# A hybrid decoder block on one core: conv gates multiplied at the convolution's results, the last mixing group in another order

## The chip, the cores and the metric

One Trainium2 chip, one core of it. The metric is the device time of one execution in microseconds (us); the time of a kernel is the median of several executions. The engines are named as in the profile: PE does the matrix products (PEld is its weight load), DVE and ACT work on tiles elementwise, POOL issues most of the kernel's own stores and reloads to and from DRAM, SP issues the loads of weights.

## What is computed

The reference is one layer over 512 tokens and a width of 2048, in float32:

```python
h = rmsnorm(x, g_mix)
cb, cc, cv, q, k, v, f_logit, gate_c, gate_a = split(h @ w_in)
conv_branch = (cb * causal_dwconv(cc * cv, conv_w)) @ w_conv_out
attn_branch = forgetting_attention(q, k, v, log_sigmoid(f_logit + b_f)) @ w_attn_out
merged = sigmoid(gate_c + b_c) * conv_branch + sigmoid(gate_a + b_a) * attn_branch
x = x + merged @ w_mix_out
h = rmsnorm(x, g_mlp)
x = x + square(relu(h @ w_ff1)) @ w_ff2
out = rmsnorm(x, g_final)
```

## The kernel before

**Products.** Every large operand is split into a rounded part and a remainder (`split`, L102: ACT writes the rounded part `th`, L103; DVE subtracts it to give `tl`, L104), and PE multiplies three of the four pairs. Most matrix products are done as seven half-size products in place of eight. A `Group` (L178) is one such product of a 512-column stretch of weights: `load` has SP fetch a quarter of the weights into one of four tiles `x0` to `x3`; `run` splits it into a `th` and a `tl` buffer (two of each, so one product ahead) and issues the matmuls, then calls what the dictionary `after` has for that product's name; `snap` is an ACT copy out of a PSUM bank and `plus` a DVE sum with one; `put(i, j, v)` takes a finished quarter (i: half of the tokens, j: half of the columns). `head` (L234) does the products A11 and A12 and puts quarter (0, 0); `tail2` (L291) does S1, S3, S2, S4 and A22 and puts (1, 1), (0, 1) and (1, 0). The weights' differences that S1 to A22 need are DVE subtractions (`sub`, L107).

**Stages around the change**, in the order of time. The gates are computed and stored to `g_d` (L757 to L777). Then come four column stretches c = 0 to 3 of the two branches. `conv_out(c)` (L871) is one `Group` with the convolution's result; before, its `put` (L873) stores each quarter to `held_d` in DRAM through POOL. `attn_out(c)` (L908) is a plain product in two chunks of 48 matmuls of 512 columns; its `cons_at` (L910) loads the attention gate `gt`, multiplies the PSUM result by it and adds that onto `merged[c]`. `bring(c)` (L891) makes the tile `merged[c]` (c below 3: the one tile `x1`), reloads the quarters from `held_d`, loads the conv gates `hg` into tiles of the ring "o" (five buffers, shared with `snap`'s copies and `gt`), and multiplies (`onto`, L882, with the DVE lines L885 and L889). `all_of(c)` (L925) makes the seven operands `M` of the mixing product from `merged[c]` (`quads`, L838), and then brings c + 1. The order is conv 0, attention 0 (with bring 0), conv 1, attention 1, conv 2, conv 3, attention 2, attention 3.

**Mixing** (L1061 to L1082) is four groups g = 0 to 3 with `M` as the token side. `Mix.put` (L984) adds x, takes squares, stores x1, and appends a `turn` (L996) to `waiting`: four PE transposes into a PSUM bank and ACT copies into `F`. `turn_waiting` (L1047) runs after certain products. In the last group the results also start the operands of the MLP: `begin_part(n, k)` (L961) reloads the first six eighths of an operand into tile `t<k>`, which is free once PE has done the products that read what lies there, `split_part` splits it, and `supply` adds a missing eighth.

**MLP, first half**: five groups begin with heads done early, and their five `tail2` come later (L1171 to L1192). The result's squares and sums are made by `sums(j)` in `put_u` (L1110): four ACT operations, five DVE operations and two POOL stores, with one buffer `r` and one `rh`, so each `sums` waits for the store of the one before. `sums(0)` is appended to `later`, and the next `tail2` runs what is in `later` (L309).

Each engine runs its instructions in the order of one list. A scheduler makes that list from the program, and the trace shows it departing from the written order (reloads and splits stand ahead of their place); an instruction that waits holds up all behind it on its engine.

Of the kernel before, what the change touches and what calls it, by code (L numbers as in the profile page):

```python
# [8 lines left out]
F32 = mybir.dt.float32  # L9
# [6 lines left out]
P = 128  # L16
# [29 lines left out]
def tile_hybrid_block(ctx: ExitStack, tc, x, g_mix, w_in, b_f, b_gate, conv_w, w_conv_out,  # L46
# [23 lines left out]
    def otile(shape, name, dt=F32):  # L70
        return main.tile(shape, dt, tag="o", name=name, bufs=5)
# [106 lines left out]
    class Group:  # L178

        def __init__(self, view, c1, c2, w, ST, mm, banks, put, scale=1.0, extra={}, after={}):
            self.extra, self.after = extra, after
            self.view, self.cs, self.w, self.ST, self.mm, self.banks = view, (c1, c2), w, ST, mm, banks
            self.put, self.scale, self.at = put, scale, {}
            self.nq = view.shape[0] // (2 * P)
# [11 lines left out]
            return [bank(i, which) for i in self.banks["abcd".index(which)]]  # L198

        def run(self, ps, n, src, first):  # L200
            hi, lo = parts([P, self.nq, self.w], SHIFT if self.w == HS else 0)
            split(src, hi, lo)
            if n in self.extra:
                self.mm(ps, self.ST(n), hi, lo, first, self.extra[n])
            else:
                self.mm(ps, self.ST(n), hi, lo, first)
            self.after.get(n, lambda: None)()
# [83 lines left out]
        def tail2(self):  # L291

            X = self.quarters((0, 1), (0, 0), (1, 1), (1, 0))
            a = self.a
            sub(X[0, 0], X[0, 1], X[0, 0])
            c = self.acc("c")
            self.run(c, "S1", X[0, 0], True)
            sub(X[0, 1], X[1, 1], X[0, 1])
            d = self.acc("d")
            self.run(d, "S3", X[0, 1], True)  # L300
            sub(X[0, 1], X[1, 1], X[0, 0])
            self.done(0, 0)
            d1 = self.snap(d, self.scale)
            self.plus(d1, c, self.scale)
            self.run(a, "S2", X[0, 1], False)
            sub(X[1, 0], X[1, 0], X[0, 1])
            self.done(0, 1)
            s2 = self.snap(a)
            while later:  # L309
                later.pop(0)()  # L310
            self.plus(d1, a, self.scale)
            self.put(1, 1, d1)
            self.run(c, "S4", X[1, 1], False)
            self.done(1, 1)
            s4 = self.snap(c, self.scale)
            self.plus(s4, a, self.scale)
            self.put(0, 1, s4)
            self.run(d, "A22", X[1, 0], False)
            self.done(1, 0)
            self.plus(s2, d)  # L320
            self.put(1, 0, s2)


    def eights(t, w=S):

# [544 lines left out]

    def conv_out(c, banks):  # L871

        def put(i, j, v):  # L873
            ts = slice(i * HS, (i + 1) * HS)
            nc.gpsimd.dma_start(out=held_d[c, 2 * j:2 * j + 2, :, ts].rearrange("k p s -> p k s"), in_=v)

        whole(Columns(w_conv_out, c * S, c * S + HS, HS, YS.get, mm_cols, tuple((b,) for b in banks), put,
                      extra={"A11": "first", "S3": "first"}))
# [3 lines left out]
    def onto(c, j, g, op):  # L882
# [3 lines left out]
        else:  # L886
            for h in range(2):
                o = merged[c][h][:, j % 2, j // 2, :]
                nc.vector.tensor_tensor(out=o, in0=o, in1=g[:, h * HS:(h + 1) * HS], op=op)  # L889

    def bring(c):  # L891

        if c < 3:
            t = main.tile([P, 2, 2, 2, HS], F32, tag="x1", name="merged")
            merged[c] = t[:, 0], t[:, 1]
            whole_of[c] = t
        else:
            merged[c] = [pm.tile([P, 2, 2, HS], F32, tag=f"f{i}", name="merged") for i in range(2)]
        for h in range(2):
            for par in range(2):  # L900
                nc.gpsimd.dma_start(out=merged[c][h][:, par], in_=held_d[c, par::2, :, h * HS:(h + 1) * HS].rearrange(
                    "j p s -> p j s"))
        for j in range(4):
            hg = otile([P, S], "hg")
            nc.gpsimd.dma_start(out=hg, in_=g_d[0, 4 * c + j])
            onto(c, j, hg, ALU.mult)

    def attn_out(c, banks, last=False, **how):  # L908

# [21 lines left out]
    M.place(4, [(n, 0) for n in ("A11", "A12", "S1", "S3")])  # L931
    M.place(6, [("S2", 0), ("S4", 0), ("A22", 0), ("A22", 1)])
    conv_out(0, lower)
    attn_out(0, upper, between={0: lambda: bring(0)})
    conv_out(1, lower)
    attn_out(1, upper, between={0: lambda: all_of(0)})
    conv_out(2, lower)
# [32 lines left out]
    class Mix:  # L970
# [25 lines left out]
        def turn(self, i, j, v):  # L996
            g = self.g
            k = 4 * g + 2 * j
            pt = bank(5 + (2 * i + j) % 3, "ptr").rearrange("p (two s) -> p two s", two=2)
            for par in range(2):  # L1000
                for t in range(2):
                    nc.tensor.transpose(pt[:, par, t * P:(t + 1) * P], v[:, t, par * P:(par + 1) * P], ident)
            gs = [gmlpT[:, k + par:k + par + 1] for par in range(2)]
            if self.last and i == 0:
                for par, n in enumerate(("A11", "A12")):
                    if n not in Q2:
                        self.missing.append((n, par, j))
                        continue
                    hi, lo = (Q2[n][:, e, 2 * g + j, :] for e in range(2))
                    nc.scalar.activation(out=hi, in_=pt[:, par, :], func=AF.Copy, scale=gs[par])  # L1010
                    nc.vector.scalar_tensor_tensor(out=lo, in0=pt[:, par, :], scalar=gs[par], in1=hi.bitcast(F32),  # L1011
                                                   op0=ALU.mult, op1=ALU.subtract)
            for par in range(2):
                nc.scalar.activation(out=self.F[i][:, par, j, :], in_=pt[:, par, :], func=AF.Copy, scale=gs[par])
            if (i, j) == (0, 1) and not self.last:
                for par, n in enumerate(("A11", "A12")):
                    self.out(n, self.F[0][:, par])
# [43 lines left out]
    for g in range(4):  # L1061
        mix = Mix(g)
        after = Steps()
        if g == 0:
            for n, n2 in zip(("A12", "S1", "S3", "S2", "S4"), ("S1", "S3", "S2", "S4", "A22")):
                after.add(n, quads3[n2])
        for n in ("A11", "S1", "S4", "A22"):
            after.add(n, turn_waiting)
        if before:
            after.add("A11", before.sums)  # L1070
        after.add("S2", mix.fourth)
        if g == 3:
            after.add("A12", lambda: begin_part("A11", 0))
            after.add("S1", lambda: split_part("A11"))
            after.add("S3", lambda: begin_part("A12", 4))
            after.add("S2", lambda: split_part("A12"), mix.supply)
            after.add("S4", lambda: begin_part("S1", 1))
        group = Group(w_mix_out, g * S, g * S + HS, HS, M.moving, mm_rows, steady(g), mix.put, after=after,
                      extra={"A12": "first"})
        group.head(True)  # L1080
        group.tail2()
        before = mix  # L1082
    def factors(common, r):

# [349 lines left out]
```

## Time and profile before

| what | value |
|---|---|
| median of 3 runs | 2480.57 us (2477.59 to 2482.46) |
| the profiled execution's own time | 2482.46 us |
| its span, first to last instruction | 2480.8 us |
| mean granted TensorE clock | 0.993 |
| DVE busy, ACT busy | 2045.3 us, 1204.1 us |

The profile is of one execution. Its own time is 1.7 us over its span, and 1.9 us over the median of the runs. Stages by the span's clock: conv and attention outputs from about 865 to 1045 us, mixing to about 1226, the heads and the five tails of the MLP's first half to about 1436.

### The profile page before, as it was taken

The numbers are of one execution on the slowest core, as the hardware profiler recorded it, in microseconds if no ns is written. First come the engines' busy times: TensorE is split into PE (matmuls) and PEld (weight loads), VectorE is DVE, ScalarE is ACT, GpSimd is POOL, SyncE is SP. The second block draws the span as 40 slices with busy tenths as digits, with TensorE's granted clock in tenths as the row PEclk, the third lists the DMA queues.
The fourth block names the chain that finished last, engine by engine and source line by source line (L and its number), as shares of the span: only waits on it lengthen the run. The fifth ranks groups of instructions, "written<-read, shape, count | busy, mean of one in ns | idle before, by whom it ended". The sixth has DMA issues, their size and how long they took to land.

```text
span 2480.8 us, 41555 instructions
## 1 busy us (share of the span) xinstructions
PE 2422.6 (98%) x17803; PEld 2277.8 (92%) x17803; DVE 2045.3 (82%) x1715; ACT 1204.1 (49%) x1223; POOL 280.6 (11%) x451
## 2 busy tenths in 40 slices
PE   8999999999999999899999899999999999999998
PEld 8999899999999988799999899999997888888886
DVE  7987777688888767687888888988978888889898
ACT  6434433445545533345665556666665333333334
POOL 0100000111111111211200000000011000100000
PEclk9999999999999999999999999999999999999999
DMA  7664544464555745746867656556587576655763
GB/s 247 187 187 150 153 136 128 132 194 149 196 196 181 255 165 175 238 142 201 274 203 268 227 210 229 176 208 230 183 290 272 197 240 213 244 185 184 257 218 104
DMA packets 296428, 497.74 MB, mean 201 GB/s; under 512 B 12060, under 2 KB 208788, under 8 KB 295860
## 3 DMA queue, kind: packets, MB, share of 16 engines
q1 hardware_dynamic: 246432, 292.64, 37.8%
q0 software_dynamic: 48944, 201.35, 21.9%
q8 instruction: 139, 2.28, 0.4%
q10 hardware_dynamic: 868, 1.10, 0.1%
q14 instruction: 45, 0.37, 0.0%
HBM read 386.51 MB, written 108.53 MB: 200 GB/s over the span
## 4 chain that ended last, share of the span: by engine, by line
PE 80%; issue 6%; DVE 6%; DMA 5%; ACT 2%; POOL 1%; DVEq 0%; SPq 0%; POOLq 0%; ACTq 0%
PE a L151 5%; PE a L167 5%; PE a L166 5%; PE a L147 5%; PE a L169 5%; PE a L149 5%; PE d L147 4%; PE d L149 4%; PE d L151 4%; PE c L147 4%; PE c L149 4%; PE c L151 3%; PE d L167 3%; PE d L166 3%; PE d L169 3%
## 5 line engine op out<-in xcount | busy, mean ns | idle before, releaser
L104 DVE TENSOR_TENSOR tl<-x,th 128x2048 fp32r<-128x2048 f32 (+1 forms) x280 | 639.4, 2287 | 167.8 <-ACT th L103 152.3
L103 ACT ACTIVATE th<-x 128x2048 fp32r<-128x2048 f32 (+1 forms) x280 | 536.8, 1918 | 483.7 <-DVE x L107 141.7
L107 DVE TENSOR_TENSOR x<-x,x 128x2048 f32<-128x2048 f32 (+1 forms) x160 | 366.0, 2287 | 26.3 <-DMA x<-in_w_in_dram 15.6
L103 ACT ACTIVATE th<-y 128x2048 fp32r<-128x2048 f32 (+1 forms) x109 | 185.1, 1700 | 268.3 <-PE a L167 138.8
L104 DVE TENSOR_TENSOR tl<-y,th 128x2048 fp32r<-128x2048 f32 (+1 forms) x109 | 219.1, 2013 | 22.9 <-ACT th L103 22.3
L147 PE MATMUL c<-S,th 128*128 128x256 f32 x912 | 213.6, 279 | 2.6 <-DVE o L110 2.6
L149 PE MATMUL c<-S,th 128*128 128x256 f32 x912 | 213.1, 278 | 0.0
L166 PE MATMUL a<-th,us 128*128 128x512 f32 x512 | 200.4, 391 | 2.2 <-ACT th L103 2.2
L167 PE MATMUL a<-th,us 128*128 128x512 f32 x512 | 200.0, 391 | 0.0
L147 PEld LDWEIGHTS c<-S,th 128*128 128x128 f32 x912 | 172.5, 189 | 3.3 <-DVE o L110 3.0
L147 PE MATMUL a<-S,th 128*128 128x256 f32 x720 | 169.5, 280 | 5.7 <-ACT th L103 5.7
L149 PEld LDWEIGHTS c<-S,th 128*128 128x128 f32 x912 | 172.6, 189 | 0.0
L149 PE MATMUL a<-S,th 128*128 128x256 f32 x720 | 167.9, 278 | 0.0
L147 PEld LDWEIGHTS a<-S,th 128*128 128x128 f32 x720 | 136.3, 189 | 6.2 <-ACT th L103 6.0
L169 PE MATMUL a<-tl,us 128*128 128x512 f32 x512 | 136.8, 389 | 0.0
L149 PEld LDWEIGHTS a<-S,th 128*128 128x128 f32 x720 | 136.5, 190 | 0.0
L149 PE MATMUL a<-A,th 128*128 128x256 f32 x544 | 126.4, 278 | 1.2 <-DVE A L1011 1.2
L147 PE MATMUL a<-A,th 128*128 128x256 f32 x544 | 126.7, 278 | 0.6 <-ACT A L1010 0.6
L149 PE MATMUL b<-A,th 128*128 128x256 f32 x544 | 126.8, 278 | 0.0
L147 PE MATMUL b<-A,th 128*128 128x256 f32 x544 | 126.7, 278 | 0.0
L147 PE MATMUL d<-S,th 128*128 128x256 f32 x544 | 126.6, 278 | 0.0
L149 PE MATMUL d<-S,th 128*128 128x256 f32 x544 | 126.0, 277 | 0.0
(369 smaller groups left out, 6084.1 us busy)
## 6 DMA issues: line engine op xcount, KB each, us to landing
x<-in_w_in_dram SPq DMA_DIRECT2D x86, 1024.0 KB, 6.0
x<-in_w_ff_dram SPq DMA_DIRECT2D x74, 1024.0 KB, 8.4
y<-in_w_ff_dram SPq DMA_DIRECT2D x64, 1024.0 KB, 7.8
us<-s_d POOLq DMA_DIRECT2D x48, 1024.0 KB, 9.6
s_d<-rh POOLq DMA_DIRECT2D x32, 896.0 KB, 5.4
s_d<-r POOLq DMA_DIRECT2D x32, 896.0 KB, 6.1
x<-in_w_mix_out_dram SPq DMA_DIRECT2D x16, 1024.0 KB, 6.2
g_d<-o POOLq DMA_DIRECT2D x32, 256.0 KB, 3.1
```

What stands on the lines that cost most here:

```text
L103: nc.scalar.activation(out=hi, in_=src, func=AF.Copy, scale=one)
L104: nc.vector.tensor_tensor(out=lo, in0=src, in1=hi.bitcast(F32), op=ALU.subtract)
L107: nc.vector.tensor_tensor(out=out, in0=a, in1=b, op=ALU.subtract)
L147: nc.tensor.matmul(o, hi[:, q, js], Sh, start=first and q == 0 and j == 0, stop=False, skip_group_check=True)
L149: nc.tensor.matmul(o, hi[:, q, js], Sl, start=False, stop=False, skip_group_check=True)
L151: nc.tensor.matmul(o, lo[:, q, js], Sh, start=False, stop=q == nq - 1, skip_group_check=True)
L166: nc.tensor.matmul(o, Sh, hi[:, q, :], start=begin and q == 0, stop=False, skip_group_check=True)
L167: nc.tensor.matmul(o, Sl, hi[:, q, :], start=False, stop=False, skip_group_check=True)
L169: nc.tensor.matmul(o, Sh, lo[:, q, :], start=False, stop=q == nq - 1, skip_group_check=True)
```

## The change

- `conv_out` loads the conv gates of its four quarters through POOL into a ring of four tiles at its start, and `put` multiplies each quarter by its gate on DVE. For c = 0 the product goes straight into the tile `merged[0]`, with no store and reload; for the others it is written over the quarter and stored to `held_d` as before. `bring` has the reload alone, and attention 0 no longer calls it.
- The last mixing group uses `tail3`, with the products in the order S1, S2, S4, S3, A22 and the quarters in the order (0, 1), (1, 1), (1, 0).
- In groups 0 to 2 the transposes run after A11, S1 and A22, no longer after S4; in group 3 after A11, S1 and S3. In group 3 `begin_part("A12", 4)`, its split and `supply` all come after S3, which is now the fourth product. The transposes of the last group's quarter (1, 1) use bank 6 in place of 5.
- `tail2` runs what is in `later` before the product S2, no longer after it.
- The mixing groups' `th` and `tl` begin at elements 0, 16, 32 and 48 of their buffers, where all began at 16. One doubled 192-column matmul at the start of each mixing group's A12 is left out.

```diff
+        def __init__(self, view, c1, c2, w, ST, mm, banks, put, scale=1.0, extra={}, after={}, shift=SHIFT):
...
-            hi, lo = parts([P, self.nq, self.w], SHIFT if self.w == HS else 0)
+            hi, lo = parts([P, self.nq, self.w], self.shift if self.w == HS else 0)
...
             self.plus(d1, c, self.scale)
+            while later:
+                later.pop(0)()
             self.run(a, "S2", X[0, 1], False)
             sub(X[1, 0], X[1, 0], X[0, 1])
             self.done(0, 1)
             s2 = self.snap(a)
-            while later:
-                later.pop(0)()
...
+        def tail3(self):
+            X = self.quarters((0, 1), (0, 0), (1, 1), (1, 0))
+            a = self.a
+            sub(X[0, 0], X[0, 1], X[0, 0])
+            c = self.acc("c")
+            self.run(c, "S1", X[0, 0], True)
+            sub(X[0, 0], X[1, 1], X[0, 0])
+            d1 = self.snap(c)
+            self.run(a, "S2", X[0, 0], False)
+            sub(X[1, 0], X[1, 0], X[0, 0])
+            self.done(0, 0)
+            s2 = self.snap(a)
+            self.plus(d1, a)
+            self.run(c, "S4", X[1, 1], False)
+            sub(X[0, 1], X[1, 1], X[0, 1])
+            self.done(1, 1)
+            s4 = self.snap(c)
+            self.plus(s4, a)
+            self.put(0, 1, s4)
+            d = self.acc("d")
+            self.run(d, "S3", X[0, 1], True)
+            self.done(0, 1)
+            self.plus(d1, d)
+            self.put(1, 1, d1)
+            self.run(d, "A22", X[1, 0], False)
+            self.done(1, 0)
+            self.plus(s2, d)
+            self.put(1, 0, s2)
...
     def conv_out(c, banks):
+        gates = {}
+        for i, j in ((0, 0), (1, 1), (0, 1), (1, 0)):
+            gates[i, j] = pc_.tile([P, 2, HS], F32, tag="hg", name="gates", bufs=4)
+            k = 4 * c + 2 * j
+            nc.gpsimd.dma_start(out=gates[i, j], in_=g_d[0, k:k + 2, :, i * HS:(i + 1) * HS].rearrange("k p s -> p k s"))
+        if c == 0:
+            place_merged(c)
+
         def put(i, j, v):
             ts = slice(i * HS, (i + 1) * HS)
-            nc.gpsimd.dma_start(out=held_d[c, 2 * j:2 * j + 2, :, ts].rearrange("k p s -> p k s"), in_=v)
+            o = whole_of[c][:, i, :, j, :] if c == 0 else v
+            nc.vector.tensor_tensor(out=o, in0=v, in1=gates[i, j], op=ALU.mult)
+            if c > 0:
+                nc.gpsimd.dma_start(out=held_d[c, 2 * j:2 * j + 2, :, ts].rearrange("k p s -> p k s"), in_=o)
...
-        for j in range(4):
-            hg = otile([P, S], "hg")
-            nc.gpsimd.dma_start(out=hg, in_=g_d[0, 4 * c + j])
-            onto(c, j, hg, ALU.mult)
...
-    attn_out(0, upper, between={0: lambda: bring(0)})
+    attn_out(0, upper)
...
-            pt = bank(5 + (2 * i + j) % 3, "ptr").rearrange("p (two s) -> p two s", two=2)
+            pt = bank((5, 6, 7, 6 if self.last else 5)[2 * i + j], "ptr").rearrange("p (two s) -> p two s", two=2)
...
-        for n in ("A11", "S1", "S4", "A22"):
+        for n in ("A11", "S1", "A22") if g < 3 else ("A11", "S1", "S3"):
             after.add(n, turn_waiting)
         if before:
             after.add("A11", before.sums)
-        after.add("S2", mix.fourth)
-        if g == 3:
+        if g < 3:
+            after.add("S2", mix.fourth)
+        else:
             after.add("A12", lambda: begin_part("A11", 0))
             after.add("S1", lambda: split_part("A11"))
-            after.add("S3", lambda: begin_part("A12", 4))
-            after.add("S2", lambda: split_part("A12"), mix.supply)
-            after.add("S4", lambda: begin_part("S1", 1))
+            after.add("S4", mix.fourth)
+            after.add("S3", lambda: begin_part("A12", 4), lambda: split_part("A12"), mix.supply)
+            after.add("A22", lambda: begin_part("S1", 1))
         group = Group(w_mix_out, g * S, g * S + HS, HS, M.moving, mm_rows, steady(g), mix.put, after=after,
-                      extra={"A12": "first"})
+                      shift=16 * g)
         group.head(True)
-        group.tail2()
+        (group.tail2 if g < 3 else group.tail3)()
```

More of the change, by code (lines that the diff above doesn't have):

```diff
@@ L178, in tile_hybrid_block @@
     class Group:
[L182 to L183 removed]
+        def __init__(self, view, c1, c2, w, ST, mm, banks, put, scale=1.0, extra={}, after={}, shift=SHIFT):
+            self.extra, self.after, self.shift = extra, after, shift
             self.view, self.cs, self.w, self.ST, self.mm, self.banks = view, (c1, c2), w, ST, mm, banks
@@ L889, in onto, with place_merged, bring @@
                 nc.vector.tensor_tensor(out=o, in0=o, in1=g[:, h * HS:(h + 1) * HS], op=op)
-    def bring(c):
+    def place_merged(c):
         if c < 3:
-            t = main.tile([P, 2, 2, 2, HS], F32, tag="x1", name="merged")
+            t = whole_of[c] = main.tile([P, 2, 2, 2, HS], F32, tag="x1", name="merged")
             merged[c] = t[:, 0], t[:, 1]
-            whole_of[c] = t
         else:
             merged[c] = [pm.tile([P, 2, 2, HS], F32, tag=f"f{i}", name="merged") for i in range(2)]
+    def bring(c):
+        place_merged(c)
         for h in range(2):
```

## The prediction

> **What bounds the kernel now.** First the page's busy line, then the table of windows, where PE's idle time and slow clock stand by stage.
>
> ```profile
> span 2480.8 us, 41555 instructions
> ...
> PE 2422.6 (98%) x17803; PEld 2277.8 (92%) x17803; DVE 2045.3 (82%) x1715; ACT 1204.1 (49%) x1223; POOL 280.6 (11%) x451
> ```
>
> PE is the bound. So an edit is worth what it takes from PE's idle time or slow clock. Columns below: window, length, busy of PE, PEld, DVE, ACT, POOL, granted clock, DMA share, GB/s.
>
> ```profile
> 907.00:955.00 48.00, 43.56 (x271) 39.27 (x270) 35.67 (x42) 17.48 (x21) 8.03 (x12) 0.96 0.50 164
> 955.00:999.00 44.00, 40.15 (x336) 39.56 (x335) 36.56 (x43) 21.01 (x26) 4.94 (x7) 0.96 0.39 126
> 999.00:1045.00 46.00, 43.83 (x194) 35.73 (x194) 31.65 (x45) 13.64 (x14) 11.78 (x18) 1.00 0.81 257
> 1045.00:1065.00 20.00, 12.07 (x62) 11.19 (x60) 15.62 (x19) 3.80 (x5) 0.71 (x1) 0.66 0.29 87
> 1065.00:1207.00 142.00, 141.44 (x1203) 140.84 (x1202) 116.52 (x88) 78.15 (x121) 31.52 (x49) 1.00 0.61 190
> 1207.00:1245.00 38.00, 34.11 (x291) 33.34 (x290) 32.05 (x31) 29.40 (x43) 7.69 (x12) 1.00 0.93 319
> 1300.00:1436.00 136.00, 127.64 (x1076) 126.53 (x1076) 117.70 (x90) 77.93 (x78) 11.31 (x21) 0.97 0.76 259
> ```
>
> Length less PE busy: 4.4, 3.9, 2.2 and 7.9 us in the branch stage and at mixing's start, 0.6 in mixing, 3.9 where mixing ends, 8.4 in the five tails. The clock adds 1.9 (0.04 x 48), 1.8, 4.1 (0.34 x 12.07 busy) and 3.8 (0.03 x 127.64). So the branch stage loses 26.2 us, the end of mixing 3.9, the tails 12.2. No edit can win more than these 42.9, apart from shortening work.
>
> The wait table of the branch stage and DVE's timeline name the cause; the bracket is the idle time before a row and what ended it.
>
> ```profile
> DVE merged L885 <- DMA merged<-held_d: 25.6, 3, 10.3
> POOL held_d L875 <- DVE o L110: 85.7, 10, 21.7
> ```
>
> ```profile
> 902.81 2.50 DVE L885 TENSOR_TENSOR merged<-merged,hg 128x512 f32<-128x512 f32 x4 [9.74 <-DMA merged<-held_d]
> ...
> 952.79 2.60 DVE L885 TENSOR_TENSOR merged<-merged,hg 128x512 f32<-128x512 f32 x4 [5.51 <-DMA merged<-held_d]
> ...
> 961.37 1.22 DVE L104 TENSOR_TENSOR tl<-y,th 128x1024 fp32r<-128x1024 f32 x1
> ...
> 1025.02 2.66 DVE L885 TENSOR_TENSOR merged<-merged,hg 128x512 f32<-128x512 f32 x4 [10.31 <-DMA merged<-held_d]
> ...
> 1032.65 2.28 DVE L104 TENSOR_TENSOR tl<-raw,th 128x2048 fp32r<-128x2048 f32 x1
> ...
> 1049.79 0.69 DVE L913 TENSOR_TENSOR gt<-pt,gt 128x512 f32<-128x512 f32 x1 [2.08 <-DMA gt<-g_d]
> ```
>
> ```profile
> 914.36 0.56 PE L147 MATMUL b<-ys,th 128*128 128x256 f32 x1 [4.44 <-ACT th L103]
> ...
> 962.64 2.07 PE L151 MATMUL b<-ys,tl 128*128 128x256 f32 x8 [3.25 <-DVE tl L104]
> ...
> 1053.78 0.58 PE L166 MATMUL a<-th,M 128*128 128x256 f32 x1 [5.62 <-ACT M L103]
> ```
>
> Three times DVE sits idle before its gate products, because the convolution's result goes through DRAM. What stands behind them (the `tl` splits at 961.37 and 1032.65, the last `merged`) comes late, and PE waits.
>
> **Gates at the convolution's results.** The loads stay 16; for c = 0 four stores and four reloads go; the products go from 12 of 512 columns and 8 of 256 to 16 of 512. They move into the conv groups, so DVE's load there counts.
>
> ```profile
> L104 DVE TENSOR_TENSOR tl<-y,th 128x1024 fp32r<-128x1024 f32 x27 | 32.9, 1220 | 5.9 <-ACT th L103 5.9
> ...
> L107 DVE TENSOR_TENSOR y<-y,y 128x1024 f32<-128x1024 f32 x11 | 13.5, 1223 | 2.4 <-DMA y<-in_w_conv_out_dram 2.1
> ...
> L885 DVE TENSOR_TENSOR merged<-merged,hg 128x512 f32<-128x512 f32 x12 | 7.7, 687 | 25.6 <-DMA merged<-held_d 25.6
> L110 DVE TENSOR_TENSOR o<-a,o 128x512 f32<-128x512 f32 x8 | 5.5, 685 | 3.9 <-ACT o L212 3.9
> ```
>
> ```profile
> 865.50:884.50 19.00, 19.00 (x170) 19.00 (x169) 14.38 (x14) 9.96 (x12) 3.81 (x6) 1.00 0.52 161
> ```
>
> A conv group has 7 splits (8.5 us), 4 subtractions (4.9) and 5 sums (3.4): 16.8 us of DVE beside 19.0 of PE. Four products of 0.69 make it 19.6, 0.6 over. By stage:
> - *907 to 955 (6.3 lost).* The reload and its wait are gone; the tile is there before attention begins. Against that, the first gate may be late:
>
> ```profile
> 864.50 1.52 POOL L785 DMA_DIRECT2D ys<-ys_d  x2
> ```
>
> ```profile
> 871.32 0.69 DVE L110 TENSOR_TENSOR o<-b,o 128x512 f32<-128x512 f32 x1 [0.94 <-PE b L151]
> ```
>
> ```profile
> hg<-g_d POOLq DMA_DIRECT2D x16, 256.0 KB, 6.4
> ...
> A<-f_d POOLq DMA_DIRECT2D x3, 768.0 KB, 6.2
> ```
>
>   Issued behind the `ys` loads at 866.0, it lands 6.4 us later at 872.4; the product could begin at 872.0. I keep 0.7 (bounds 0 and 2) and count 5.6 won. The Trainium skill (SBUF — State Buffer, "The DMA setup-cost knee") fits a transfer as 2 us plus bytes over 436 GB/s, an estimate of 2.6 us here; by that the gate lands at 868.6 and the 0.7 is nothing. The median row, measured under this stage's traffic, decides for me.
> - *955 to 999 (5.7 lost).* The 2.60 us of products and, where the attention gate's products run in the idle 5.51, more than that leave the split at 961.37. Of the stall of 3.25 at most 0.65 stays; the overflow of conv 2 and conv 3, back to back, is 1.2; 1.1 for a dip of the clock behind what stays. Keep 3.0, win 2.7.
> - *999 to 1045 (2.2 lost).* 2.66 us of products leave, and `gt` times PSUM fills part of the 10.31. Keep 0.2, win 2.0.
> - *1045 to 1065 (12.0 lost).* The chain to `merged[3]` loses the 2.66 at 1025.02, eight half products (about 2.8 us at the row's pace) and the 2.08 at 1049.79, where `gt` waited because four `hg` held the ring "o" of five; with some 2.7 us of `gt` products done in the idle time that is 10.2 us. PE waited 5.62 and about 1.9, and comes 2.0 sooner itself: 9.5. Covered, but only just. Keep 3.0, win 9.0.
>
> Together 19.3 us. Bounds: 26.2 if nothing stays; about 12 if the wait is inherited (rival one).
>
> A stall that stays can cost its length again in clock:
>
> ```profile
> 1346.96 0.39 PE L147 MATMUL c<-S,th 128*128 128x256 f32 x1 [2.02 <-DVE o L110]
> ```
>
> ```profile
> 1347.90:1351.30 3.40, 3.40 (x19) 3.40 (x18) 3.40 (x3) 1.60 (x2) 0.53 (x1) 0.50 0.98 299
> ```
>
> 2.02 us idle, and the clock is at half for 3.4 us (1.7 lost). The Trainium skill (TensorE: Matmul & The Clock Gate, "Why this matters for your kernels") allows idle gaps up to about 3 us between bursts; by it, my kept stalls would cost no clock, 1.1 less. This row speaks against relying on that.
>
> **End of mixing.** With S4 third, quarter (0, 1) is put and turned one product (48 matmuls, 5.6 us) before A22, so the MLP's A11 finds its last columns.
>
> ```profile
> 1220.26 0.63 PE L1002 MATMUL ptr<-ident,o 128*128 128x128 f32 x4 [1.61 <-DVE o L110]
> ...
> 1230.22 0.38 PE L147 MATMUL a<-A,th 128*128 128x256 f32 x1 [0.64 <-ACT A L1010]
> ...
> 1232.65 0.38 PE L149 MATMUL a<-A,th 128*128 128x256 f32 x1 [1.24 <-DVE A L1011]
> ```
>
> ```profile
> 1206.53 0.57 POOL L964 DMA_DIRECT2D A<-f_d  x1 [8.07 <-PE d L169]
> ```
>
> The two waits of A11 (1.9) go, and of the 1.61 a part. Against that, the reload for A12 waits for S3 (row at 1206.53), which is now fourth: issue, 6.2 us, and splits of some 1.5 on ACT and 1.8 on DVE make 9.5 us, and A22 and A11 cover 11.2. If the split stands ahead of A22's `th` on ACT, PE waits all of that but the DVE part, some 8 us; a reload queued in POOL behind it waits too, but those are needed much later. Win 2.5 (bounds: 3.9 won, 8 lost).
>
> **Tails.** `sums(0)` moves one product up: four ACT operations, five on DVE, two stores and the next fetch on POOL. All of it is now written ahead of S2's split.
>
> ```profile
> 1341.23 0.64 ACT L1113 ACTIVATE r<-c 128x512 f32<-128x512 f32 x1 [2.05 <-DMA s_d<-r]
> ...
> 1379.22 0.63 ACT L1113 ACTIVATE r<-c 128x512 f32<-128x512 f32 x1 [6.08 <-DMA s_d<-r]
> ```
>
> ACT already waits for buffer `r` here. Moving the sums up doesn't free `r` earlier, but gives the store until the next `sums(1)` a product more. DVE is near its limit (117.70 of 136). I take 0. Bounds: 8 of the 12.2 won; 3 us lost in each of two tails (S2's split moved behind a landing) for 6.
>
> **The rest.** Four matmuls less at 142.00/1203 = 0.12 us: 0.5. Transposes after A22 in place of S4: hidden, since the sum they wait for is older by then; without that cover, 1.6 for each group (row at 1220.26). The bank: 0. Offsets: products read 256 columns at 279 ns alike from weights at offset 16 and from whole tiles:
>
> ```profile
> L166 PE MATMUL c<-th,M 128*128 128x256 f32 x112 | 27.0, 279 | 0.0
> ```
>
> ```profile
> L147 PE MATMUL c<-S,th 128*128 128x256 f32 x912 | 213.6, 279 | 2.6 <-DVE o L110 2.6
> ```
>
> I take 0; half a nanosecond on 1008 matmuls either way is 0.5.
>
> **Sum.** 19.3 + 2.5 + 0 + 0.5 = 22.3. From the profiled execution's 2482.46 that is 2460.2; its time is 1.9 over the median 2480.57, so 2458.
>
> **Rivals.**
> 1. *The sums inherit the wait.* `merged` + `gt` also needs the reload, so for c = 1 and 2 DVE is held as before. For: the reload starts no sooner, as tile `x1` is free only after the step before. Against: DVE has the `gt` products to do first, and PE finishes them late. Then the first stage wins 5.6, the next two some 3, the last 4: with the rest 15.5, 2465.
> 2. *The tails get worse*: 6 lost as above, 2464.
> 3. *Slower: the gates come late.* POOL is one line, and its stores wait for DVE (85.7 us in 10). If each gate's load stands behind the store of the quarter before, it is issued one product (2.7 us) ahead and lands 6.4 later: 3.7 us of DVE at each of 16 products, 59 us; less 22.3, about 2517. It decides from 1.4 us for each product (22.3/16). Against: the four loads stand ahead of the group's own stores.
> 4. *It doesn't do what it says*: the list puts the same waits elsewhere (DVE 82% busy); some 2479.
> 5. *More than forecast*: nothing kept, and half of the tails' bound, 33.2 won: 2447.
>
> **How the numbers follow.** Forecast 0.56, rivals 0.18, 0.09, 0.06, 0.06, 0.05. A measurement of this kernel tells some 0.2% (5 us) from no change. Faster: 0.56 + 0.18 + 0.09 + 0.05 = 0.88; same 0.06; slower 0.06. The range goes from rival five to past one with an unlucky end of mixing: 2446 to 2471, which leaves out rivals three and four and little else.
>
> **What would show it.** Right: no gate product waits on `merged<-held_d`; PE's idle time in the branch stage and at mixing's start falls from 18.4 to some 5, the clock's dips there mostly go; A11 of the MLP starts without a wait; the tails lose some 12 again. Wrong: L885 with `gt` waits 5 to 10 us on the reload; the products in `put` wait on `hg<-g_d`; ACT waits on `A<-f_d` with A22's split behind it; S2 in the tails starts late behind L1113.

## The result and the profile after

The changed kernel takes 2480.88 us (median of 18 executions, 2474.03 to 2486.5), the kernel before 2478.18 on the same chip (18 executions). The ratio is 1.0009, 95% interval 0.9999 to 1.0018: no gain, where 2458 was forecast.

The page's busy line, then the windows of the profiled execution after, laid on its own stages (columns as in the prediction's table of windows).

```profile
span 2481.2 us, 41527 instructions
...
PE 2425.0 (98%) x17799; PEld 2280.6 (92%) x17799; DVE 2044.8 (82%) x1711; ACT 1201.6 (48%) x1223; POOL 277.7 (11%) x443
```

```profile
907.00:955.00 48.00, 48.00 (x325) 43.84 (x324) 39.51 (x47) 20.52 (x24) 8.70 (x12) 1.00 0.53 175
955.00:999.00 44.00, 42.84 (x327) 40.24 (x326) 40.36 (x46) 20.81 (x25) 10.90 (x15) 1.00 0.59 194
999.00:1033.60 34.60, 34.60 (x154) 28.39 (x153) 21.47 (x26) 10.02 (x11) 4.33 (x6) 1.00 0.77 247
1033.60:1052.00 18.40, 14.55 (x97) 13.85 (x96) 15.56 (x21) 7.37 (x8) 0.72 (x1) 0.81 0.05 16
1052.00:1195.00 143.00, 142.85 (x1216) 142.38 (x1216) 117.16 (x88) 78.84 (x122) 32.36 (x50) 1.00 0.64 200
1195.00:1227.00 32.00, 25.24 (x196) 25.04 (x196) 23.88 (x22) 20.71 (x34) 5.44 (x9) 0.84 0.88 295
1300.00:1440.00 140.00, 122.21 (x1007) 120.00 (x1005) 108.51 (x86) 72.58 (x75) 9.68 (x18) 0.97 0.68 228
```

The branch stage was mended: PE loses 0, 1.2 and 0 us in the first three windows, and 3.85 idle with 2.8 of slow clock (0.19 x 14.55) at mixing's start: 7.8 where it was 26.2. But the end of mixing now has 6.8 us idle at a clock of 0.84, and the tails 17.8 idle. The start of the same matmuls in both traces shows where the gain went:

| first matmul of | before | after | won so far |
|---|---|---|---|
| conv 0's A11 | 865.5 | 866.0 | -0.4 |
| mixing's A11 | 1045.6 | 1033.6 | 12.0 |
| last mixing group's S1 | 1195.0 | 1177.1 | 17.9 |
| MLP's second head, A11 | 1240.8 | 1227.2 | 13.6 |
| third `tail2`'s S1 | 1328.2 | 1317.1 | 11.1 |
| fifth head's A12 | 1365.0 | 1359.6 | 5.4 |
| sixth group's A12 | 1440.9 | 1440.3 | 0.6 |

17.9 us are won up to the last mixing group, then nearly all of it is given back: 4.3 there (17.9 to 13.6), and 13.0 in the tails (13.6 to 0.6).

**The wait that rival one named came, and PE did not feel it there.** The wait table and DVE's timeline of after:

```profile
DVE merged L926 <- DMA merged<-held_d: 12.5, 2, 8.3
```

```profile
873.50 0.68 DVE L914 TENSOR_TENSOR merged<-o,gates 128x512 f32<-128x512 f32 x1
...
947.22 0.69 DVE L926 TENSOR_TENSOR merged<-merged,gt 128x512 f32<-128x512 f32 x1 [4.12 <-DMA merged<-held_d]
...
1013.93 0.69 DVE L926 TENSOR_TENSOR merged<-merged,gt 128x512 f32<-128x512 f32 x1 [8.34 <-DMA merged<-held_d]
```

L914 is the new product, L926 the old L885. The first gate makes nothing wait, and no other product waits for one. (Rival three's order did come: in after POOL issues the store of a quarter at 957.41 and the next gates at 958.14, but each such load is for the convolution group after.) The sums wait for the reload in two places of three (12.5 us, before 25.6), and PE is 0 to 1.2 us idle in these windows. Whether the second wait is part of the 3.85 at mixing's start is not shown: from 1013.93 to 1038.6 DVE is busy for 22.6 of 24.7 us, and the `M` that PE then waits for stands behind that work.

**The end of mixing.** POOL, ACT, DVE and PE of after in the order of time:

```profile
1194.15 0.57 POOL L1004 DMA_DIRECT2D S<-f_d  x1 [10.51 <-PE c L169]
```

```profile
1193.25 1.92 ACT L103 ACTIVATE th<-x 128x2048 fp32r<-128x2048 f32 x1 [2.98 <-issue]
1195.08 0.58 ACT L212 ACTIVATE o<-c 128x512 f32<-128x512 f32 x1
1201.96 1.48 ACT L103 ACTIVATE S<-S 128x1536 fp32r<-128x1536 f32 x1 [6.30 <-DMA S<-f_d]
...
1204.81 1.90 ACT L103 ACTIVATE th<-x 128x2048 fp32r<-128x2048 f32 x1
```

```profile
1203.48 1.76 DVE L104 TENSOR_TENSOR S<-S 128x1536 fp32r<-128x1536 f32 x1 [4.65 <-ACT S L103]
1205.15 0.48 DVE L1051 SCALAR_TENSOR_TENSOR A<-ptr,cols,A 128x256 fp32r<-128x256 f32 x1
1205.55 0.42 DVE L104 TENSOR_TENSOR A<-f,A 128x256 fp32r<-128x256 f32 x1
1205.88 0.69 DVE L110 TENSOR_TENSOR o<-d,o 128x512 f32<-128x512 f32 x1
```

```profile
1206.71 0.55 PE L166 MATMUL d<-th,M 128*128 128x256 f32 x1 [6.76 <-ACT th L103]
```

With S4 third, the tile into which the MLP's S2 operand is reloaded is free sooner, so its reload and split move up in the lists: ACT and DVE both wait for it. PE's last row names `th`, but A22's own `th` is the row at 1193.25; the one that ends at 1206.71 is that of the MLP's first A11. A22 adds onto bank d, which DVE must first have read: in `tail3` S3's result is not copied out by ACT but summed by DVE (`o<-d,o`, until 1206.57), and that sum stands in DVE's list behind the split. The profile puts a wait for two things down to the one that came last.

**The tails.** ACT and PE of after around the fifth head's A12:

```profile
1340.31 0.63 ACT L1154 ACTIVATE r<-c 128x512 f32<-128x512 f32 x1 [7.01 <-DMA s_d<-r]
...
1356.80 0.94 ACT L1149 ACTIVATE r<-o 128x256 f32<-128x256 f32 x2 [5.32 <-DMA s_d<-r]
1357.64 1.89 ACT L103 ACTIVATE th<-x 128x2048 fp32r<-128x2048 f32 x1
```

```profile
1359.59 0.58 PE L147 MATMUL b<-A,th 128*128 128x256 f32 x1 [4.12 <-ACT th L103]
```

ACT waits for r's store, A12's `th` stands behind, PE stalls (again at 1440.33, 4.62). And the DMA view of the window 1290 to 1430, before and after (KB each, median us from issue to landing):

```profile
x<-in_w_ff_dram SPq DMA_DIRECT2D x19, 1024.0 KB, 7.1
```

```profile
x<-in_w_ff_dram SPq DMA_DIRECT2D x18, 1024.0 KB, 8.4
```

The weights land 1.3 us later; r's stores too (8.0 before, 9.0 after). So there were two readings to tell apart: the chain through the one buffer r, or the traffic.

### The profile page after: what moved, and what is told of

Same layout as the page of the kernel before. It is cut to its first block, busy times and chain, and to the rows that moved or that the text cites. A ratio compares the mean times of both kernels' runs of the same rounds, so it can differ in the third digit from the quotient of the medians.

```text
span 2481.2 us, 41527 instructions
## 1 busy us (share of the span) xinstructions
PE 2425.0 (98%) x17799; PEld 2280.6 (92%) x17799; DVE 2044.8 (82%) x1711; ACT 1201.6 (48%) x1223; POOL 277.7 (11%) x443
## 3 DMA queue, kind: packets, MB, share of 16 engines
q0 software_dynamic: 48304, 199.25, 21.7%
## 5 line engine op out<-in xcount | busy, mean ns | idle before, releaser
L147 PE MATMUL b<-A,th 128*128 128x256 f32 x544 | 130.2, 283 | 8.7 <-ACT th L103 8.7
L149 PE MATMUL b<-A,th 128*128 128x256 f32 x544 | 129.7, 282 | 0.0
```

The source lines that it names most:

```text
L147: nc.tensor.matmul(o, hi[:, q, js], Sh, start=first and q == 0 and j == 0, stop=False, skip_group_check=True)
L149: nc.tensor.matmul(o, hi[:, q, js], Sl, start=False, stop=False, skip_group_check=True)
```

## The experiments

Each kernel was measured beside the kernel before, whose medians there were 2480.1 to 2481.5; the ratio is to that. e6, e9, e10 and e14 leave out or replace stores, as said with them.

| kernel | median us | ratio, 95% interval |
|---|---|---|
| e1 sums back after S2 | 2462.90 | 0.9923 (0.9901 to 0.9945) |
| e2 old mixing end | 2477.02 | 0.9986 (0.9972 to 1.0001) |
| e3 both back | 2463.64 | 0.9932 (0.9912 to 0.9951) |
| e4 gates alone | 2463.61 | 0.9926 (0.9905 to 0.9947) |
| e5 sums back, end mended | 2461.29 | 0.9922 (0.9908 to 0.9936) |
| e6 remainder from rh | 2476.62 | 0.9983 (0.9972 to 0.9995) |
| e7 sums ahead alone | 2496.10 | 1.0062 (1.0049 to 1.0075) |
| e8 sums(1) behind A12 | 2477.91 | 0.9988 (0.9977 to 0.9998) |
| e9 ahead, no stores | 2458.07 | 0.9911 (0.9893 to 0.9929) |
| e10 after S2, no stores | 2449.24 | 0.9872 (0.9855 to 0.9890) |
| e11 sums after S4, end mended | 2454.61 | 0.9897 (0.9879 to 0.9914) |
| e12 end mended, sums ahead | 2475.51 | 0.9975 (0.9964 to 0.9986) |
| e13 A12 first | 2475.34 | 0.9976 (0.9966 to 0.9986) |
| e14 one store | 2461.39 | 0.9922 (0.9906 to 0.9938) |
| e15 sums after S4, end as changed | 2458.43 | 0.9908 (0.9893 to 0.9922) |
| e16 both remedies | 2452.14 | 0.9884 (0.9869 to 0.9898) |

A single ratio is sure to some 0.1 to 0.2% (3 to 5 us), a difference of two of them to some 4 to 6. Differences below are of medians where nothing else is said. Beside them stands, where it helps, the length of a stage in the profiled executions, one for each kernel: "the tails' stretch" is from the A11 of the MLP's second head to the sixth group's A12, 200.1 us before and 213.1 after.

### Undoing the parts

e1 puts the sums back:

```diff
             self.plus(d1, c, self.scale)
-            while later:
-                later.pop(0)()
             self.run(a, "S2", X[0, 1], False)
...
             s2 = self.snap(a)
+            while later:
+                later.pop(0)()
```

> The changed kernel with one edit undone: tail2 runs what is in `later` (the squares and sums of the quarter (1, 0) of the group before) after the product S2 again. Theory A (the sums ahead of S2 cost the tails some 13 us, through the store of the one buffer r, behind which the next head's rounded weights stand on ACT): the waits of L1149 on s_d<-r fall from 5.3 and 5.4 us to under 1, PE's stalls of 4.1 and 4.6 us at the heads' A12 go, the tails lose about 13 us over the matmuls' pace instead of 26, time about 2468. Rival B (the tails can't take work sooner, because loads and stores bound them, and hand back whatever was won before them): the tails still lose about 26, time 2481 within 2. Rival C (the tails lose because the mixing's end leaves its reloads late): the same as B in time, and the stalls come from reloads.

e2 puts the last mixing group back, and its bank 5 (e3 both):

```diff
-        for n in ("A11", "S1", "A22") if g < 3 else ("A11", "S1", "S3"):
+        for n in ("A11", "S1", "A22") if g < 3 else ("A11", "S1", "S4", "A22"):
...
+            after.add("S3", lambda: begin_part("A12", 4))
+            after.add("S2", lambda: split_part("A12"), mix.supply)
+            after.add("S4", lambda: begin_part("S1", 1))
...
-        (group.tail2 if g < 3 else group.tail3)()
+        group.tail2()
```

> The changed kernel with the last mixing group as before (order S1, S3, S2, S4, A22, its steps and turns at their old places, bank 5 again). Theory A (in the new order the reload of an S operand is issued when S4, now third, is done, and its split stands ahead of A22's rounded weights on ACT): ACT's wait of 6.3 us on S<-f_d at the group's end is no longer ahead of A22, PE's stall of 6.9 us and the slow clock of 2.8 behind it go, the two waits of the MLP's first A11 (1.9 us) come back; the heads start 7 us sooner than in the changed kernel against the mixing's start, time about 2474. Rival B (the tails hand it back): the heads start 7 sooner, the end does not, time 2481 within 2.

> Both undone: what stays of the change is the conv gates, the turns in groups 0 to 2, the offsets and the matmul left out. Theory A (the two losses stand apart and add up): 2481 less 13 less 7, about 2461. Rival B (what is won is handed back in the tails): 2476 to 2481. Between the two, some 2468, would mean that each loss covers part of the other.

e4 is the kernel before with the new `conv_out`, `place_merged` and `bring`, and `attn_out(0, upper)` without `bring(0)`:

> The kernel before with the conv gates' edit alone. Theory A: the 18 us won up to the mixing's last group stay to the end, since the tails as before have room for them: 2478 less 18, about 2460. Rival B (the end is bound by loads or stores of the tails): 2473 to 2478. Against the run with both undone it tells the turns, the offsets and the matmul left out: 0.5 us by my count.

e7 is the kernel before with the move of `later` alone:

> The kernel before with the one edit that tail2 runs `later` ahead of S2. Theory A (the edit has its own price, whatever comes before it): 2479 and some 15 to 18, 2494 to 2497. Rival B (it only keeps the tails from being faster than their loads and stores, so that it takes back what the gates won and no more): 2479 within 2. Rival D (in the kernel before it costs nothing, since the stores of r were not yet in the way): the same 2479, and no waits of ACT on s_d<-r over 3 us ahead of a head's A12.

The gates alone win 16.5 us (2463.61 against 2480.12), near the 17.9 that the trace shows; turns, offsets and the matmul left out add nothing that shows (e3 and e4 agree to 0.03). The sums ahead of S2 cost 18.0 (after against e1), 13.4 with the old mixing end (e2 against e3) and 14.6 on the kernel before (e7): a price of their own, and not a hand-back, which refutes rivals B and C. The tails' stretch says the same with less scatter: 211.7 to 214.9 us in the four kernels with all stores and the sums ahead (after, e2, e7, and e12 below), 198.5 to 200.9 in the five with the sums after S2 (before, e1, e3, e4, and e5 below). So the price is some 12 to 18 us. The old mixing end wins 3.9 with the sums ahead (e2) and nothing with the sums back (e3 against e1).

### The mixing end mended

e5 is e1 with the reloaded operands' splits held, in the lists of ACT and DVE, behind the first head's `th` and the sum of bank d:

```diff
-            self.plus(d1, d)
+            marks["sum"] = nc.vector.tensor_tensor(
+                out=d1, in0=d[0].rearrange("p (b c) -> p b c", b=2), in1=d1, op=ALU.add).ins
...
+    heads[0].head(False, lambda: (begin_part("S3", 2), marks.update(first=marks["A11"])))
...
-            split_part(n)
+            with tc.issue_after(marks["sum"]), tc.issue_after(marks["first"]):
+                split_part(n)
```

> As the kernel with the sums back after S2 (2462.9 us), and in the new mixing end the split of the reloaded S operands is kept, in the engines' lists, behind DVE's sum of bank d with S3 and behind the rounded weights of the MLP's first A11. Theory A (A22 adds onto the bank d, so it must wait until DVE has read S3's result out of it, and that sum stood behind the remainder of an operand whose reload had not landed): A22 starts when S3 ends, the 5.7 us of stall and 2.3 of slow clock in that kernel go, the MLP's A11 starts 8 us sooner; 2455 if it stays to the end. Rival B (the tails hand back what the mixing's end wins: with the old end the heads began 7 us sooner and the time was 2463.6): the heads start sooner and the time is 2461 to 2465. Rival C (A22 waits for its rounded weights): the stall stays, since these stood ahead of the operand's split already.

DVE and PE of e5:

```profile
1195.30 0.69 DVE L348 TENSOR_TENSOR o<-d,o 128x512 f32<-128x512 f32 x1 [0.73 <-PE d L170]
...
1204.88 1.76 DVE L104 TENSOR_TENSOR A<-A 128x1536 fp32r<-128x1536 f32 x1 [3.24 <-ACT A L103]
...
1206.89 0.68 DVE L111 TENSOR_TENSOR o<-d,o 128x512 f32<-128x512 f32 x1
```

```profile
1210.43 0.66 PE L1044 MATMUL ptr<-ident,o 128*128 128x128 f32 x4 [2.30 <-DVE o L111]
```

The sum now follows S3 at once, and A22 starts at 1196.14 without the stall: the cause is shown, and rival C is refuted. But the next sum stands behind the next reloaded operand (1204.88), and PE waits 2.30 for it. The time came out as rival B said, 2461 and not 2455, so the price of the end is less than the 8 us of stall and slow clock that e1 has there. Two more measure it beside other tails: e12 is after with this edit, e15 is after with the sums after S4 (the edit is shown with e11 below):

> The changed kernel with the mended mixing end alone, the sums ahead of S2. If the losses stand apart: the stall of 6.9 us and the slow clock go, 2481 less 8, 2473. If the tails take most of what comes sooner (as with the sums back, where 8 us at the heads' start became 1.6 at the end): 2477 to 2481.

> The changed kernel with the sums after S4 and the end of mixing as changed, with its stall of some 6 us and slow clock of 2 to 3. With the mended end it was 2454.6. Theory A (a stall of PE is lost for good where the tails have nothing to give back): 2454.6 and 6 to 8, 2461 to 2463. Rival B (the tails swallow what comes sooner): 2454 to 2457.

The mend wins 1.6 (e1 to e5), 5.4 (after to e12) and 3.8 us (e15 to e11): some 4, where two ratios can tell some 4 to 6 (by ratios it is 0.2, 8.4 and 2.7 us). In the profiled executions the stretch from the last mixing group's S1 to the second head's A11 is 43.5 to 45.6 us with the mended end, 49.1 to 50.5 with the end as changed and 45.6 to 48.5 with the old one. So in its own place the mend wins some 4 to 7 us. In time e12 and e15 came out between their two expectations.

### Buffer or traffic

e6 is after with r out of the stores' way and all the traffic: both stores take the rounded part, and the remainder is never stored. The edit acts in all groups, also those behind the five tails:

```diff
-            nc.gpsimd.dma_start(out=s_d[g // 2][:, 1, q], in_=r)
+            nc.gpsimd.dma_start(out=s_d[g // 2][:, 1, q], in_=h.bitcast(F32))
```

> The changed kernel, with the remainders of the sums not stored: the second store of each sums takes the rounded part from rh again, so r is free as soon as DVE has subtracted and no store reads it; the traffic is the same, and the remainders of the operands of the second product are wrong. Theory A (the chain through r's store costs the tails their 13 to 18 us): ACT's waits of L1149 and L1154 on s_d<-r go, the heads' A12 stall no more, 2481 less 13 to 18, 2463 to 2468. Rival B (the wait moves on to rh, whose next writing L1165 then waits for two stores, with the same rounded weights behind it): 2476 to 2481. Rival C (what costs is the later weights: S2's remainder later, so the weight tiles come free later): the r waits go and the time stays within 3 of 2481.

e8 and e13 are after with the second sums behind the next head's A12; only e13 has the line with `issue_after`, which holds them behind A12's rounded weights on ACT:

```diff
-                sums(1)
+                if g < AHEAD:
+                    late.append(lambda: sums(1))
+                else:
+                    sums(1)
...
             self.run(b, "A12", X[1, 0], True)
+            while late:
+                with tc.issue_after(marks["A12"]):
+                    late.pop(0)()
```

> The changed kernel with the second sums of each of the five groups (quarter (0, 1)) run behind the product A12 of the next head, or at the start of the next tail2, in place of at once; the sums of `later` stay ahead of S2. The rounded weights of A12 then stand ahead of the writing of r on ACT. Theory A (the stalls at the heads' A12 are the rounded weights held behind r's store): the stalls of 4.3 and 4.8 us and the slow clock behind them (1.6 and 2.2) go, 2481 less 13, 2468, or less if the waits show again at S1. Rival C (the later weights cost): 2477 to 2481.

> The changed kernel with the second sums of the first five groups run behind the next head's A12 and kept, in ACT's list, behind A12's rounded weights (in the earlier try of this, one of their operations still stood ahead). Theory A (these rounded weights behind r's store are the main price): the two stalls of 4.4 and 4.9 us and the slow clock of 1.6 and 2.2 behind them go, 2481 less 10 to 13, 2468 to 2471. Theory F (the stalls are where the lateness shows, not where it comes from: weights that load slowly beside the stores, and S2's splits behind the sums): the loss comes up at other products, 2475 to 2479.

e9 (from after) and e10 (from e1) leave out both stores of the first five groups, e14 (from after) the remainder's alone; the second product reads later groups' parts of the same size in place of what is not stored. The edit of e9:

```diff
-            nc.gpsimd.dma_start(out=s_d[g // 2][:, 0, q], in_=h.bitcast(F32))
-            nc.gpsimd.dma_start(out=s_d[g // 2][:, 1, q], in_=r)
+            if g >= AHEAD:
+                nc.gpsimd.dma_start(out=s_d[g // 2][:, 0, q], in_=h.bitcast(F32))
+                nc.gpsimd.dma_start(out=s_d[g // 2][:, 1, q], in_=r)
...
-                nc.gpsimd.dma_start(out=t[:, e].bitcast(F32), in_=s_d[seg][:, e, :, 2 * k:2 * k + len(names)])
+                nc.gpsimd.dma_start(out=t[:, e].bitcast(F32), in_=s_d[seg + 3 if seg < 3 else seg][:, e, :, 2 * k:2 * k + len(names)])
```

> The changed kernel without the stores of the sums in the first five groups and the sixth's counterpart unread: those groups' sums are computed and not stored, and the second product reads the parts of later groups in their place (same size, other values). It is to be read against the next kernel, the same with the sums after S2. Theory A (the price of the sums ahead of S2 is all in the stores: r waiting for them, and the weights' loads beside them): both kernels come to the same time within 3 us, some 2453 to 2460. Theory E (the price is in the order on ACT and DVE: S2's rounded weights and remainder behind nine operations of the sums): this one stays 10 to 18 us slower than the next.

> The same without stores, and `later` run after S2 as before. Theory A: as the kernel above within 3 us, and some 3 to 9 below the one with stores (2462.9), since the tails still lost 12.5 us there, part of it in waits behind r. Theory E: 10 to 18 us below the kernel above.

> The changed kernel without the store of the remainder in the first five groups (the second product reads later groups' remainders in place of these): r is never held by a store, and the traffic of the sums is halved. With r free and all the traffic it was 2476.6, with no store 2458.1. Theory A (r is what counts; the traffic doesn't): 2474 to 2478. Theory F (the traffic counts): about half way, 2465 to 2469.

The wait tables of the tails (1290 to 1430; total us, times, longest) of after, e6, e13, e14 and e1 in this order show what took the place of what:

```profile
ACT r L1154 <- DMA s_d<-r: 16.4, 3, 7.0
...
DVE x L107 <- DMA x<-in_w_ff_dram: 7.8, 3, 3.5
...
ACT r L1149 <- DMA s_d<-r: 5.3, 1, 5.3
```

```profile
DVE x L107 <- DMA x<-in_w_ff_dram: 15.8, 4, 5.6
...
ACT rh L1165 <- DMA s_d<-rh: 4.7, 1, 4.7
```

```profile
ACT r L1162 <- DMA s_d<-r: 12.6, 3, 6.9
...
DVE x L108 <- DMA x<-in_w_ff_dram: 11.0, 3, 6.3
```

```profile
DVE x L107 <- DMA x<-in_w_ff_dram: 9.8, 3, 3.9
```

```profile
ACT r L1149 <- DMA s_d<-r: 12.8, 4, 4.1
...
ACT r L1154 <- DMA s_d<-r: 9.4, 4, 4.2
...
DVE x L107 <- DMA x<-in_w_ff_dram: 1.4, 2, 1.2
```

ACT waits for r's store 21.7 us in after and 22.2 in e1 (whose waits at L1149 I had expected to fall under 1), and e1 is 18.0 faster: the sum of those waits is no measure of their price. With r free (e6) they are gone, but DVE waits 15.8 for weights (7.8 in after, 1.4 in e1), and the time falls by only 4.3. That is not the tails alone: their stretch is 9.2 us shorter than in after (203.9), and what is behind them 5.8 longer (1046.6 against 1040.8; 1039.1 to 1044.9 in all others), where the edit acts too. In e8 one writing of r still stood ahead of A12's `th` (1348.28, 4.99 of wait), so it decided nothing; in e13 none does, and PE's stall comes up at A12's remainder instead:

```profile
1357.89 1.38 PE L152 MATMUL b<-A,tl 128*128 128x256 f32 x5 [3.04 <-DVE tl L104]
```

That wins 5.5 us (4.1 in the tails' stretch), and not 10 to 13. So the buffer, on which I had put the whole price, is some 4 to 9 of it. The DMA view (1290 to 1430) of e1, e6, e14, e9 and e10:

```profile
x<-in_w_ff_dram SPq DMA_DIRECT2D x18, 1024.0 KB, 7.0
```

```profile
x<-in_w_ff_dram SPq DMA_DIRECT2D x17, 1024.0 KB, 8.3
```

```profile
x<-in_w_ff_dram SPq DMA_DIRECT2D x18, 1024.0 KB, 6.8
```

```profile
x<-in_w_ff_dram SPq DMA_DIRECT2D x19, 1024.0 KB, 5.6
```

```profile
x<-in_w_ff_dram SPq DMA_DIRECT2D x19, 1024.0 KB, 5.5
```

Same bytes, another place: with the sums ahead a weight load takes 8.3 to 8.4, with the sums back 7.0, and without the stores 5.6 and 5.5, wherever the sums are. One store left out (e14, r never in the way) takes it to 6.8 and wins 15.2 us on e6 (5.3 in the tails' stretch, which is the fairer measure, as e6 loses behind it). The two orders with and without the stores:

| | both stores | no stores | the stores' price |
|---|---|---|---|
| sums ahead of S2, median (after, e9) | 2480.9 | 2458.1 | 22.8 |
| sums after S2, median (e1, e10) | 2462.9 | 2449.2 | 13.7 |
| sums ahead of S2, tails' stretch | 213.1 | 192.0 | 21.1 |
| sums after S2, tails' stretch | 198.5 | 186.5 | 12.0 |

By both measures the stores are some 9 us dearer with the sums ahead (by the medians sure to some 8; the stretch is of one execution each, but kernels alike in these stages agree in it within some 3 us). What is left is the order on the engines (with the fetch on POOL, which moves along): 8.8 by the medians, sure to some 6, and 5.5 by the tails' stretch. So of the 14.6 to 18.0 between after and e1 some 9 is the stores, and 5 to 9 the order on ACT and DVE. Within the 9, the buffers that the stores hold and their traffic beside the weights' loads are not cleanly parted: no run frees r alone with the sums after S2, and e6 moves the hold on to rh (4.7 us of ACT's wait). e6 speaks for the traffic: no store holds r there, and still the loads take 8.3 and DVE waits 15.8 us for them. Theory F had the direction; its half way for e14 (2465 to 2469) was too little.

### The other way, and a better kernel

e11 is e5 with `later` run one product later, between S4's copy and its sum; e16 adds e13's edit:

```diff
-            while later:
-                later.pop(0)()
             self.plus(d1, a, self.scale)
...
             s4 = self.snap(c, self.scale)
+            while later:
+                later.pop(0)()
             self.plus(s4, a, self.scale)
```

> The kernel with the mended mixing end (2461.3 us), and `later` run one product later still, after S4. If a product earlier costs 15 us because of the distance of two stores of one buffer: later, sums(0) comes closer to the sums(1) behind it, whose writing of r waits longer, with the next head's A12 behind it: 5 to 15 us slower, 2466 to 2476. If what counts is only that the sums stand clear of S2's split: as the kernel it is made from, 2459 to 2464.

> The kernel with the mended end and the sums after S4 (2454.6), and the second sums behind A12's rounded weights as in the first run here. Theory A: ACT's wait for r no longer has anything of PE's behind it, but in that kernel A12's rounded weights stood ahead already in the place looked at, so 2452 to 2455. Theory F: the second sums come a product later, nearer to the next sums of the same buffer: 2455 to 2460.

Both my expectations for e11 were wrong: later still is better, by 6.7 (2454.61 against 2461.29). Ahead of S2, after S2, after S4 is 2475.5, 2461.3, 2454.6 with the mended end, and 214.9, 200.9, 195.1 in the tails' stretch. e16 is the fastest of those that keep all stores, 2452.14, 1.2% under before. Its end of mixing and its tails, beside the rows of after above:

```profile
1195.00:1227.00 32.00, 29.80 (x256) 29.36 (x254) 28.30 (x30) 28.83 (x40) 9.78 (x11) 1.00 0.88 309
1300.00:1440.00 140.00, 133.82 (x1160) 132.77 (x1159) 125.44 (x96) 85.60 (x86) 10.70 (x20) 1.00 0.72 249
```

2.2 us idle where after has 6.8, 6.2 in the tails where after has 17.8, and the clock at full in both.

## Why the prediction was wrong, step by step

- **What bounds the kernel**: right. PE's idle time and slow clock by stage told what could be won.
- **Gates at the convolution's results**: right. 19.3 was forecast, 17.9 shows in the trace, and 16.5 in the time of e4. PE's idle time in these stages fell from 18.4 to 5.0, as the prediction said it would. The gates' loads took 4.2 us (median, 3.0 the least), between the 6.4 and the 2.6 that the prediction weighed, and the first, issued at 869.61 and not at 866.0, still made nothing wait. The kept 0.7 and 3.0 of the first two windows were 0 and 1.2; the kept 3.0 at mixing's start was 6.6 (2.89 of it a wait for ACT's `M`, the rest after it and the clock).
- **Rival one** happened in its mechanism, without the price that it put on it: DVE's waits of 4.12 and 8.34 us leave PE 0 to 1.2 us idle in their windows. Whether the second is part of the 6.6 is not shown.
- **End of mixing**: failed. I took 2.5 won. The bound of 8 lost was the size, for another wait than I named: not A22's `th` behind A12's reload, but DVE's sum of bank d behind S2's operand, because `tail3` sums S3's result where `tail2` copies it. The trace lost 6.8 there and 2.9 of clock (half of 5.9 us, 1206.7 to 1212.6), and against before it lost 4.3 of what had been won; in time the end is some 4 worse than a mended one. With the wait mended this stretch is 0 to 5 us shorter than with the old end, where 2.5 was forecast.
- **Tails, "I take 0"**: the step that decided. It cost 13.0 in the traces' table and 13 to 18 in time, more than twice the bound of 6. I had seen that ACT waits for r, and argued that r isn't freed sooner. Two things were left out: what the sums' operations ahead of S2's split cost on ACT and DVE (5 to 9), and that two stores of 896 KB each, issued a product earlier, cost some 9 more than before, by the buffer and beside the weights' loads, which land in 8.4 us where they took 7.1. Rival two had the sign, but the price of 6 and one cause.
- **The rest**, 0.5: not to be told from 0 (e3 and e4).
- The sum by what the traces show: 17.9 won, 4.3 lost at mixing's end and 13.0 in the tails, 0.6 left at the sixth group's A12, and nothing at the end of the span (2481.2 against 2480.8). The forecast had 22.3 there.

The clock did as in the row of before that I relied on. PE's row and the window of after:

```profile
1331.06 0.39 PE L147 MATMUL a<-S,th 128*128 128x256 f32 x1 [2.02 <-ACT th L103]
```

```profile
1332.10:1335.50 3.40, 3.40 (x18) 3.40 (x17) 3.40 (x3) 1.20 (x2) 0.00 (x0) 0.50 0.97 268
```

2.02 us idle, and from 1 us behind it half the clock for 3.4 us, 1.7 more lost. The Trainium skill (TensorE: Matmul & The Clock Gate, "Why this matters for your kernels") allows gaps up to about 3 us; this trace does not agree with that. But the length of a gap alone doesn't decide: in before the clock stayed at full behind gaps of 2.17 (1034.99) and 2.41 us (1417.54).

**Open.** How the 5 to 9 us of order divide between ACT and DVE, and how the 9 of the stores divide between the buffer and the traffic. In medians the second store costs 15.2 (e6 against e14) and the first 3.3 (e14 against e9), but in the tails' stretch 5.3 and 6.6, so that they are uneven is not shown. r in two buffers was not tried.

## What to carry to other kernels

A block of work moved up a product takes its stores along: ask what loads they will fall on, and what splits its operations now stand ahead of in each engine's list, before taking it as free. A sum in place of a copy out of PSUM ties the next product's start to another engine's queue, so look what that queue waits for. When a stall goes away at a named wait and the time doesn't, look for the same lateness at the next product before believing the name.

## What the runs showed of the hardware

- In the tails a weight load of 1 MB took 5.5 us (median) without the stores of the sums (e10), 7.0 with these stores and the sums after S2 (e1), and 8.4 with them a product earlier (after). The Trainium skill (SBUF — State Buffer, "The DMA setup-cost knee") gives an estimate of 4.4 us, 2 us and 1 MB over 436 GB/s; the nearest row here is the 5.5 without stores.
